# Second feed-forward product: the weight differences of Winograd's seven products made in other tiles

## The chip, the cores and the metric

The kernel runs on one core of a Trainium2 chip. The metric is the device time of one execution in microseconds (us), as the median over several runs. The engines that matter here are PE (TensorE, matrix products), ACT (ScalarE), DVE (VectorE), and SP (SyncE), which issues all the transfers. Each engine takes its instructions in a fixed order that was settled when the program was built, and an instruction that waits for another engine holds up everything behind it on its own engine.

## The reference, cut to what matters

One layer of a transformer-like trunk on 512 tokens of width 2048. Its last step is a gated feed-forward network, in float32:

```
h = rms_norm(x, norm2_g) * (1.0 + sc2) + sh2
gate, up = jnp.split(h @ w_ffn_in, 2, axis=-1)          # D_FF = 5632
x = x + g2 * ((jax.nn.silu(gate) * up) @ w_ffn_out)     # 5632 -> 2048
```

The change lies in the last product, `... @ w_ffn_out`, which is called the second product below. It takes the last 440 us or so of the execution.

## The kernel before

**Split numbers.** PE multiplies in a rounded 32-bit format. To keep float32 accuracy, each weight tile is split into a high and a low part: ACT copies it with rounding (`hi`, line 220), then DVE subtracts the copy from the tile (`lo`, line 221). Each block then needs three matmuls: high by high, low by high, high by low. The high tiles and the low tiles each have three rotating buffers, and every fourth split goes to a spare pair inside the tile `opsB`. So rows with `opsB` as a weight are splits like the others.

**Seven products instead of eight.** The second product is done by Winograd's form of Strassen's scheme: the four quarters of the weight block, y[0] to y[3], are combined to seven operands, and each is multiplied by a matching combination of the activations. Those were prepared earlier, lie in DRAM as `opd`, and come in as `opsA`, `opsB` and `opsC`. The order of the seven is `ORDER = (2, 1, 7, 6, 4, 5, 3)`. "Product 7" below is the one with that number, which comes third. Trace names count the place in the order from 0 and then the first block of a pair: `wfo6_2_0l` is unit 6, third product (7), blocks 0 and 1, low part.

**Units.** The 22 blocks of the inner dimension are cut into six chunks of 3, 3, 4, 4, 4 and 4 blocks, each done for two halves of the output columns. That gives 12 units, numbered 0 to 11. From unit 4 on a product is two pairs of blocks, or 24 matmuls.

**Sums.** Product 2 collects in the accumulators `foB`, products 7 and 4 in `foC`, products 1, 6, 5 and 3 all in the same two accumulators `foA` (one for each token half, called foA0 and foA1). After a product its result goes into the output tile `O`: mostly ACT copies it out (line 1210) and DVE adds the copy (line 1211). For product 3 DVE adds straight from `foA` (line 1275). The next unit's product 1 overwrites `foA`, so it may begin only when that add is done.

**Weight tiles and differences.** y[0] and y[2] of a unit come into a pool of four rotating buffers (`wfo`). y[1] and y[3] come into `yraw`, of which there is one for unit 0 and one for all the others. `T2` is a fifth tile of the same size, also one for all units after the first. `load_y` issues these loads on SP. y[1] and y[3] of the next unit have to wait until the present unit's last reader of the same tile is done. Before the change DVE makes four differences, each for pairs of blocks:

| for product | difference | line |
|---|---|---|
| 7 | y[0] becomes y[1] - y[0], all blocks ahead of the first split | 1254 |
| 7 | y[1] becomes y[3] - y[1] | 1190 |
| 6 | T2 becomes y[3] - y[0], with the new y[0] | 1190 |
| 4 | y[2] becomes y[2] - T2 | 1190 |

Product 1 takes the original y[0], so the first difference, which overwrites it, waits for product 1's split.

**What sets the order.** A scheduler in the framework places each engine's instructions by priority and by what it expects to be ready. Splits and differences have raised priority (`high_priority(offset=AHEAD)`), ACT's copies out of the accumulators have more; the adds into `O` have the ordinary one, so they go where the list has a gap.

Of the kernel before, what the change touches and what calls it, by code (L numbers as in the profile page):

```python
# [26 lines left out]
CHUNKS = (3, 3, 4, 4, 4, 4)  # L27
ORDER = (2, 1, 7, 6, 4, 5, 3)
AHEAD = 300
# [100 lines left out]
def trunk(ctx, tc, a):  # L130
    nc = tc.nc
    V, S, G = nc.vector, nc.scalar, nc.gpsimd
# [790 lines left out]
    for i, hs in enumerate(halves):  # L923
# [15 lines left out]
        y = rb[:, hs]  # L939
# [47 lines left out]
    for j in range(HALF):  # L987
        V.tensor_sub(block(0, 0, j), block(0, 1, j), block(0, 0, j))
        t2 = ft.tile([P, HT], F32, tag="t", name=f"t2_{j}")
# [34 lines left out]
    def place(n):  # L1024
        n %= 11
        return places[0][:, n] if n < 4 else places[1][:, n - 4] if n < 7 else places[2][:, n - 7]

    def load_op(c, q):
        if c < len(CHUNKS):
            nc.sync.dma_start(place(7 * c + q)[:, 0:CHUNKS[c]].bitcast(F32),  # L1030
                              opd[c][:, ORDER[q] - 1].rearrange("p n (h t) -> p n h t", h=2))

    def load_y(u, b):
        if u == len(units):
            return
        c, i = units[u]
        n = CHUNKS[c]
        t = raw_tile([P, n, T], f"wfo{u}_{b}") if b % 2 == 0 else yraw[u > 0][:, b // 2, 0:n]
        nc.sync.dma_start(t, a["w_fo"][i, b][:, starts[c]:starts[c] + n])
        blocks[u][b] = t  # L1040
# [142 lines left out]
    def multiply(out, c, q, raw, first, u, sums):  # L1183
        n = CHUNKS[c]
        x = place(7 * c + q)
        for k0 in range(0, n, 2):
            w = min(2, n - k0)
            with tc.high_priority(offset=AHEAD):
                for d, e, g in sums:
                    V.tensor_sub(*(t[:, k0:k0 + w] for t in (d, e, g)))  # L1190
            whi, wlo = split(raw[:, k0:k0 + w], [P, w, T], f"wfo{u}_{q}_{k0}")
            for j in range(2):
                js = slice(j * P, j * P + P)
                for kk in range(w):
                    k = k0 + kk
                    flags = dict(stop=False, skip_group_check=True)
                    PE.matmul(out[j], x[:, k, 0, js], whi[:, kk], start=first and k == 0, **flags)
                    PE.matmul(out[j], x[:, k, 0, js], wlo[:, kk], start=False, **flags)
                    flags["stop"] = k == n - 1
                    PE.matmul(out[j], x[:, k, 1, js], whi[:, kk], start=False, **flags)  # L1200

    def onto(dst, src, first):
        if first:
            with tc.high_priority(offset=2 * AHEAD):
                S.copy(dst, src)
            return
        t = cond[:, taps[0] % 4 * T:taps[0] % 4 * T + T]
        taps[0] += 1
        with tc.high_priority(offset=2 * AHEAD):
            S.copy(t, src)  # L1210
        V.tensor_add(dst, dst, t)
# [14 lines left out]
    def some_out(n):  # L1226
        for _ in range(min(n, len(outs))):
            emit_out(*outs.pop(0))

    for u, (c, i) in enumerate(units):  # L1230
        def dst(th, j, dh):
            return O[:, 2 * th + j, dh * 1024 + i * T:dh * 1024 + i * T + T]

        def ready(th, dh):
            if c == last_c:
                outs.extend((8 * dh + 4 * i + m, th) for m in range(4))

        first, final = c == 0, c == last_c
        if final and i == 0:
            for g in range(4):  # L1240
                nc.sync.dma_start(place(7 * c + 7 + g).bitcast(F32).rearrange("p n h t -> p n (h t)"), x1d[:, 4 * g:4 * g + 4])
        y = blocks[u]
        t2 = (T2 if u else yraw[0][:, 2])[:, 0:CHUNKS[c]]
        load_y(u + 1, 2)
        load_y(u + 1, 0)
        for q, p in enumerate(ORDER):
            out = {2: B[i], 7: C, 4: C}.get(p, A)
            raw = {2: y[2], 1: y[0], 7: y[1], 6: t2, 4: y[2], 5: y[0], 3: y[3]}[p]
            sums = {7: [(y[1], y[3], y[1])], 6: [(t2, y[3], y[0])], 4: [(y[2], y[2], t2)]}.get(p, ())
            if p == 7:  # L1250
                with tc.high_priority(offset=AHEAD):
                    for k0 in range(0, CHUNKS[c], 2):
                        ks = slice(k0, min(k0 + 2, CHUNKS[c]))
                        V.tensor_sub(y[0][:, ks], y[1][:, ks], y[0][:, ks])
            multiply(out, c, q, raw, p in (1, 7) or p == 2 and first, u, sums)
            if final:
                some_out(3)
            for j in range(2):
                if p == 1:
                    onto(dst(0, j, 0), A[j], first)  # L1260
                    if final:
                        V.tensor_add(dst(0, j, 0), B[i][j], dst(0, j, 0))
                elif p == 7:
                    onto(dst(1, j, 1), C[j], first)
                elif p == 6:
                    onto(dst(1, j, 0), A[j], first)
                elif p == 4:
                    V.tensor_add(dst(1, j, 0), C[j], dst(1, j, 0))
                elif p == 5:
                    onto(dst(1, j, 1), A[j], False)  # L1270
                elif p == 3:
                    if first:
                        S.copy(dst(0, j, 1), A[j])
                    else:
                        V.tensor_add(dst(0, j, 1), A[j], dst(0, j, 1))
            if p == 1:
                ready(0, 0)
                if final:
                    slots += [t[:, h * HT:h * HT + HT] for t in B[i] for h in range(2)]
            elif p in (4, 5, 3):  # L1280
                ready(*{4: (1, 0), 5: (1, 1), 3: (0, 1)}[p])
            if p == 7:
                load_y(u + 1, 1)
            if p == 3:
                load_y(u + 1, 3)
            if u == 0 and q == 6:
                places.append(hp.tile([P, 4, 4, 2, HT], F32R, tag="hhi", name="opsC"))
            if q < 4 and i == (c == 0):
                load_op(c + 1, q)
            if i == 1 and 1 <= q < 4:  # L1290
                load_op(c + 1, q + 3)
# [60 lines left out]
```

## Time and profile before

| | us |
|---|---|
| runs | 2299.24, 2299.24, 2306.46 (median 2299.24) |
| the profiled execution, its own time | 2301.37 |
| the profiled execution, span from the first to the last instruction | 2299.2 |
| PE busy | 2249.4 (98%) |
| DVE busy | 1917.8 (83%) |
| ACT busy | 1160.6 (50%) |

The span is the time from the first to the last instruction, and the execution's own time is 2.2 us more. PE is busy nearly throughout, so a change shows in the time only where it lengthens or shortens one of the few stretches in which PE waits, or adds matmuls. A timeline row gives the start and the length in us, the engine, the line, the operation, the tiles (buffer numbers left out), the shapes and the count. In brackets stands the idle time before it and what ended it. L93 is the helper that issues every matmul. Matmuls overlap: a row of one 128x512 matmul shows 0.39 us, while they follow each other every 0.227 us.

### The profile page before, as it was taken

The numbers are of one execution on the slowest core, as the hardware profiler recorded it, in microseconds if no ns is written. First come the engines' busy times: TensorE is split into PE (matmuls) and PEld (weight loads), VectorE is DVE, ScalarE is ACT, GpSimd is POOL, SyncE is SP. The second block draws the span as 40 slices with busy tenths as digits, with TensorE's granted clock in tenths as the row PEclk, the third lists the DMA queues.
The fourth block names the chain that finished last, engine by engine and source line by source line (L and its number), as shares of the span: only waits on it lengthen the run. The fifth ranks groups of instructions, "written<-read, shape, count | busy, mean of one in ns | idle before, by whom it ended". The sixth has DMA issues, their size and how long they took to land.

```text
span 2299.2 us, 35729 instructions
## 1 busy us (share of the span) xinstructions
PE 2249.4 (98%) x14171; PEld 2050.2 (89%) x14171; DVE 1917.8 (83%) x2566; ACT 1160.6 (50%) x2015; POOL 10.7 (0%) x25
## 2 busy tenths in 40 slices
PE   7999899999999999999999999999999999999999
PEld 6899899888888788999999999999999977778787
DVE  8887779999888865699899988888888778888888
ACT  4316666565655522564454445454545544544453
POOL 0000000000000000000000000000000000000000
PEclk9999999999999999999999999999999999999999
DMA  9885546853322386346555645454443486665452
GB/s 368 319 317 218 174 145 227 304 183 111 128 93 74 130 303 214 105 151 225 189 204 185 220 143 175 143 174 143 150 160 129 166 314 232 238 220 213 154 200 76
DMA packets 114978, 437.69 MB, mean 190 GB/s; under 512 B 9822, under 2 KB 58236, under 8 KB 76796
## 3 DMA queue, kind: packets, MB, share of 16 engines
q1 hardware_dynamic: 114812, 435.42, 53.0%
q8 instruction: 111, 1.82, 0.3%
q14 instruction: 55, 0.45, 0.1%
HBM read 386.61 MB, written 48.77 MB: 189 GB/s over the span
## 4 chain that ended last, share of the span: by engine, by line
PE 77%; DVE 13%; DMA 3%; issue 3%; ACT 3%; SPq 0%; DVEq 0%; ACTq 0%
PE ffA L93 18%; PE foA L93 9%; PE ffC L93 9%; PE sbp L93 7%; PE wo L93 7%; PE foC L93 4%; PE ffB L93 4%; PE st L93 4%; PE hgf L93 4%; PE hgq L93 3%; PE hgg L93 3%; DMA opd<-fhi 1%; DVE ada L180 1%; DVE yraw L1190 1%; PE l L93 1%
## 5 line engine op out<-in xcount | busy, mean ns | idle before, releaser
L180 DVE SCALAR_TENSOR_TENSOR ada<-ada,cond 128x2048 f32<-128x2048 f32 x95 | 216.8, 2286 | 54.5 <-DMA ada<-in_w_ada 54.3
L93 PE MATMUL ffA<-opD,ff_3h 128*128 128x256 f32 x512 | 93.9, 284 | 1.8 <-ACT u L1018 1.7
L93 PE MATMUL ffA<-opB,ff_6h 128*128 128x256 f32 x512 | 94.1, 284 | 1.0 <-ACT ff_6h L220 1.0
L93 PE MATMUL ffB<-opA,ff_2h 128*128 128x256 f32 x512 | 93.5, 283 | 0.0
L93 PE MATMUL ffC<-opC,ff_4h 128*128 128x256 f32 x512 | 93.5, 283 | 0.0
L93 PE MATMUL ffA<-opC,ff_5h 128*128 128x256 f32 x496 | 90.7, 283 | 0.8 <-ACT b L1018 0.8
L93 PE MATMUL ffA<-opA,ff_1h 128*128 128x256 f32 x496 | 90.6, 283 | 0.0
L93 PE MATMUL ffC<-opB,ff_7h 128*128 128x256 f32 x496 | 90.6, 283 | 0.0
L221 DVE TENSOR_TENSOR wfo_0l<-wfo,wfo_0h 128x1024 fp32r<-128x1024 f32 x48 | 58.7, 1224 | 37.9 <-ACT wfo_0h L220 37.5
L93 PEld LDWEIGHTS ffA<-opD,ff_3h 128*128 128x128 f32 x512 | 79.7, 192 | 2.4 <-ACT u L1018 2.4
L93 PEld LDWEIGHTS ffA<-opB,ff_6h 128*128 128x128 f32 x512 | 80.1, 193 | 1.3 <-ACT ff_6h L220 1.2
L93 PEld LDWEIGHTS ffC<-opC,ff_4h 128*128 128x128 f32 x512 | 79.7, 192 | 0.0
L93 PEld LDWEIGHTS ffB<-opA,ff_2h 128*128 128x128 f32 x512 | 79.7, 192 | 0.0
L220 ACT CAST wfo_0h<-wfo 128x1024 fp32r<-128x1024 f32 x48 | 50.6, 1054 | 57.5 <-PE foA L93 50.4
L1092 ACT CAST fhi<-forms 128x512 fp32r<-128x512 f32 (+1 forms) x63 | 43.6, 692 | 68.5 <-DMA opd<-fhi 59.2
L93 PEld LDWEIGHTS ffA<-opC,ff_5h 128*128 128x128 f32 x496 | 77.2, 192 | 1.0 <-ACT b L1018 1.0
L93 PEld LDWEIGHTS ffC<-opB,ff_7h 128*128 128x128 f32 x496 | 77.3, 192 | 0.0
L93 PEld LDWEIGHTS ffA<-opA,ff_1h 128*128 128x128 f32 x496 | 77.2, 192 | 0.0
L93 PE MATMUL ffA<-opB,ff_6l 128*128 128x256 f32 x256 | 72.7, 284 | 0.0
L93 PE MATMUL ffC<-opC,ff_4l 128*128 128x256 f32 x256 | 72.4, 283 | 0.0
L93 PE MATMUL ffA<-opD,ff_3l 128*128 128x256 f32 x256 | 72.4, 283 | 0.0
L93 PE MATMUL ffB<-opA,ff_2l 128*128 128x256 f32 x256 | 72.4, 283 | 0.0
(1646 smaller groups left out, 7764.6 us busy)
## 6 DMA issues: line engine op xcount, KB each, us to landing
ada<-in_w_ada SPq DMA_DIRECT2D x95, 1024.0 KB, 5.2
wfo<-in_w_fo SPq DMA_DIRECT2D x16, 1024.0 KB, 5.9
yraw<-in_w_fo SPq DMA_DIRECT2D x16, 1024.0 KB, 4.8
fix<-in_w_fix SPq DMA_DIRECT2D x14, 1024.0 KB, 5.6
opd<-forms SPq DMA_DIRECT2D x44, 256.0 KB, 4.3
opd<-fhi SPq DMA_DIRECT2D x42, 256.0 KB, 4.3
opsC<-opd SPq DMA_DIRECT2D x10, 1024.0 KB, 5.1
opsA<-opd SPq DMA_DIRECT2D x9, 1024.0 KB, 7.2
```

What stands on the lines that cost most here:

```text
L93: self.engine.matmul(out, lhsT, rhs, **kw)
L180: V.scalar_tensor_tensor(w, w, 1.0, row, op0=ALU.mult, op1=ALU.mult, accum_out=col)
L220: S.copy(hi, r)
L221: V.tensor_sub(lo, r, hi.bitcast(F32))
L1092: S.copy(hi, R[:, q])
L1190: V.tensor_sub(*(t[:, k0:k0 + w] for t in (d, e, g)))
```

## The change

Other tiles hold the differences. For product 7, y[3] - y[1] goes to T2 rather than over y[1], and then y[1] becomes y[1] - y[0]. For product 6, y[0] becomes y[3] - y[1], with the new y[1]. For product 4, y[2] becomes y[2] - y[0]. Product 5 takes y[1] where it took y[0]. The operands have the same values as before. There are four differences as before, but the loop that made the first of them for all blocks ahead is gone: both of product 7's are now made pair by pair inside `multiply`. Since y[1] is now read until product 5's split, the next unit's y[1] is loaded after product 5 rather than after product 7.

```diff
-            raw = {2: y[2], 1: y[0], 7: y[1], 6: t2, 4: y[2], 5: y[0], 3: y[3]}[p]
-            sums = {7: [(y[1], y[3], y[1])], 6: [(t2, y[3], y[0])], 4: [(y[2], y[2], t2)]}.get(p, ())
-            if p == 7:
-                with tc.high_priority(offset=AHEAD):
-                    for k0 in range(0, CHUNKS[c], 2):
-                        ks = slice(k0, min(k0 + 2, CHUNKS[c]))
-                        V.tensor_sub(y[0][:, ks], y[1][:, ks], y[0][:, ks])
+            raw = {2: y[2], 1: y[0], 7: t2, 6: y[0], 4: y[2], 5: y[1], 3: y[3]}[p]
+            sums = {7: [(t2, y[3], y[1]), (y[1], y[1], y[0])], 6: [(y[0], y[3], y[1])], 4: [(y[2], y[2], y[0])]}.get(p, ())
             multiply(out, c, q, raw, p in (1, 7) or p == 2 and first, u, sums)
...
-            if p == 7:
+            if p == 5:
                 load_y(u + 1, 1)
```

The scheduler answers with another order on the engines. In the rows below numbers tell tiles of one name apart, and the five lines of code taken out shift later line numbers: the add of line 1275 is line 1270 afterwards.

DVE at the head of unit 6, before, from product 1's first low part on; `O<-foA0` is the add of unit 5's product 3 from the first accumulator:

```order
L221 TENSOR_TENSOR wfo6_1_0l_20133<-wfo6_0_19844,wfo6_1_0h_20132 128x1024
L1275 TENSOR_TENSOR O_18741<-foA0_18742,O_18741 128x512
L1254 TENSOR_TENSOR wfo6_0_19844<-yraw_18716,wfo6_0_19844 128x1024
L221 TENSOR_TENSOR wfo6_1_2l_20149<-wfo6_0_19844,wfo6_1_2h_20148 128x1024
L1190 TENSOR_TENSOR yraw_18716<-yraw_18716 128x1024
L1254 TENSOR_TENSOR wfo6_0_19844<-yraw_18716,wfo6_0_19844 128x1024
L1190 TENSOR_TENSOR T2_18739<-yraw_18716,wfo6_0_19844 128x1024
L221 TENSOR_TENSOR wfo6_2_0l_20173<-yraw_18716,wfo6_2_0h_20172 128x1024
```

and with the change, from the same instruction:

```order
L221 TENSOR_TENSOR wfo6_1_0l_20133<-wfo6_0_19844,wfo6_1_0h_20132 128x1024
L1190 TENSOR_TENSOR T2_18739<-yraw_18716 128x1024 x2
L221 TENSOR_TENSOR wfo6_1_2l_20149<-wfo6_0_19844,wfo6_1_2h_20148 128x1024
L1190 TENSOR_TENSOR yraw_18716<-yraw_18716,wfo6_0_19844 128x1024
L221 TENSOR_TENSOR wfo6_2_0l_20172<-T2_18739,wfo6_2_0h_20171 128x1024
L1190 TENSOR_TENSOR yraw_18716<-yraw_18716,wfo6_0_19844 128x1024
L1190 TENSOR_TENSOR wfo6_0_19844<-yraw_18716 128x1024
L221 TENSOR_TENSOR opsB_18712<-T2_18739,opsB_18712 128x1024
L1190 TENSOR_TENSOR wfo6_0_19844<-yraw_18716 128x1024
L221 TENSOR_TENSOR wfo6_3_0l_20210<-wfo6_0_19844,wfo6_3_0h_20209 128x1024
L1190 TENSOR_TENSOR wfo6_2_19842<-wfo6_2_19842,wfo6_0_19844 128x1024 x2
L1270 TENSOR_TENSOR O_18741<-foA0_18742,O_18741 128x512
```

The add from foA0, second before, now comes after 13 instructions of 128x1024. Units 8 and 10 have the same order as unit 6. In units 5, 7 and 9 the first `T2` stands ahead of product 1's first low part, one of product 4's differences comes before product 6's low part, and 12 instructions from that low part on precede the add.

PE at the same place, before, from the end of product 2 to the beginning of product 7:

```order
L93 MATMUL foB01_18745<-opsB_18712,opsC_18951 128x512 x6
L93 MATMUL foA0_18742<-wfo6_1_0h_20132,opsA_18700 128x512
L93 MATMUL foA0_18742<-wfo6_1_0l_20133,opsA_18700 128x512
L93 MATMUL foA0_18742<-wfo6_1_0h_20132,opsA_18700 128x512 x2
L93 MATMUL foA0_18742<-wfo6_1_0l_20133,opsA_18700 128x512
L93 MATMUL foA0_18742<-wfo6_1_0h_20132,opsA_18700 128x512
L93 MATMUL foA0_18742<-wfo6_1_2h_20148,opsA_18700 128x512
L93 MATMUL foA0_18742<-wfo6_1_2l_20149,opsA_18700 128x512
L93 MATMUL foA0_18742<-wfo6_1_2h_20148,opsA_18700 128x512 x2
L93 MATMUL foA0_18742<-wfo6_1_2l_20149,opsA_18700 128x512
L93 MATMUL foA0_18742<-wfo6_1_2h_20148,opsA_18700 128x512
L93 MATMUL foC_18748<-wfo6_2_0h_20172,opsA_18700 128x512
```

and with the change, from the end of product 2 to the beginning of product 1:

```order
L93 MATMUL foB01_18745<-opsB_18712,opsC_18951 128x512 x6
L93 MATMUL foC_18748<-wfo6_2_0h_20171,opsA_18700 128x512
L93 MATMUL foC_18748<-wfo6_2_0l_20172,opsA_18700 128x512
L93 MATMUL foC_18748<-wfo6_2_0h_20171,opsA_18700 128x512 x2
L93 MATMUL foC_18748<-wfo6_2_0l_20172,opsA_18700 128x512
L93 MATMUL foC_18748<-wfo6_2_0h_20171,opsA_18700 128x512 x2
L93 MATMUL foC_18748<-wfo6_2_0l_20172,opsA_18700 128x512
L93 MATMUL foC_18748<-wfo6_2_0h_20171,opsA_18700 128x512 x2
L93 MATMUL foC_18748<-wfo6_2_0l_20172,opsA_18700 128x512
L93 MATMUL foC_18748<-wfo6_2_0h_20171,opsA_18700 128x512
L93 MATMUL foC_18748<-opsB_18712,opsA_18700 128x512 x12
L93 MATMUL foA0_18742<-wfo6_1_0h_20132,opsA_18700 128x512
```

Product 7 now goes ahead of all of product 1; before, product 1's half in foA0 went first. It is so in units 3 and 5 to 11.

DVE near the end of unit 0, before, where `wfo0_5_0l` is the first low part of unit 0's product 5 and `forms42` still belongs to the stage before:

```order
L1093 TENSOR_TENSOR forms42_18475<-forms42_18475,cond_72 128x512 x2
L1093 TENSOR_TENSOR forms42_18475<-forms42_18475,cond_72 128x768
L221 TENSOR_TENSOR wfo0_5_0l_18895<-wfo0_0_18705,wfo0_5_0h_18894 128x1024
L221 TENSOR_TENSOR wfo0_5_2l_18911<-wfo0_0_18705,wfo0_5_2h_18910 128x512
L221 TENSOR_TENSOR wfo0_6_0l_18925<-yraw0_18707,wfo0_6_0h_18924 128x1024
```

and with the change:

```order
L1093 TENSOR_TENSOR forms42_18475<-forms42_18475,cond_72 128x512 x2
L1093 TENSOR_TENSOR forms42_18475<-forms42_18475,cond_72 128x768
L1190 TENSOR_TENSOR T2_18739<-yraw_18716 128x1024
L1190 TENSOR_TENSOR T2_18739<-yraw_18716 128x512
L1190 TENSOR_TENSOR yraw_18716<-yraw_18716,wfo1_0_18751 128x1024
L1190 TENSOR_TENSOR yraw_18716<-yraw_18716,wfo1_0_18751 128x512
L221 TENSOR_TENSOR wfo0_5_0l_18894<-yraw0_18707,wfo0_5_0h_18893 128x1024
L221 TENSOR_TENSOR wfo0_5_2l_18910<-yraw0_18707,wfo0_5_2h_18909 128x512
L221 TENSOR_TENSOR wfo0_6_0l_18925<-yraw0_18707,wfo0_6_0h_18924 128x1024
```

Unit 1's four differences for product 7 now stand ahead of unit 0's product 5, and the first of them waits for the loads of unit 1's y[1] and y[3]. On SP the loads of y[1] for units 2 and later move back, past the next two `wfo` loads and up to three loads of activations, until they stand close to the load of y[3].

## The prediction, made before the changed kernel was run

> **What bounds the kernel now.** I read the page first, then PE's waits in the second product, then the timeline at one unit boundary.
>
> ```profile
> span 2299.2 us, 35729 instructions
> PE 2249.4 (98%) x14171; PEld 2050.2 (89%) x14171; DVE 1917.8 (83%) x2566; ACT 1160.6 (50%) x2015; POOL 10.7 (0%) x25
> ...
> PE 77%; DVE 13%; DMA 3%; issue 3%; ACT 3%; SPq 0%; DVEq 0%; ACTq 0%
> ```
>
> PE is the bound. No matmul is added or removed, so the time moves only by what PE waits. From the list of waits, second product alone:
>
> ```profile
> PE foA L93 <- ACT O L1205: 3.6, 1, 3.6
> PE foC L93 <- DVE wfo_0l L221: 2.4, 2, 1.3
> PE foC L93 <- DVE wfo_2l L221: 1.6, 3, 0.5
> PE foC L93 <- DVE opsB L221: 1.6, 3, 0.5
> ...
> PE foC L93 <- ACT wfo_0h L220: 0.3, 1, 0.3
> ```
>
> Columns: total, times, longest. All but the first are product 7 (foC) waiting for its low parts: two longer waits, in units 3 and 4, and six of 0.53, one in each of units 5 to 10. Together 5.9 us. That is what the change can win; the 3.6 us lie at unit 0's product 6, which it does not touch. Now the head of unit 6:
>
> ```profile
> 2048.50 0.39 PE L93 MATMUL foA<-wfo_2h,opsC 128*128 128x512 f32 x1
> 2049.78 1.23 DVE L221 TENSOR_TENSOR wfo_0l<-wfo,wfo_0h 128x1024 fp32r<-128x1024 f32 x1 [1.01 <-ACT wfo_0h L220]
> 2050.93 0.68 DVE L1275 TENSOR_TENSOR O<-foA,O 128x512 f32<-128x512 f32 x1
> 2051.22 0.39 PE L93 MATMUL foB<-wfo_0h,opsC 128*128 128x512 f32 x1
> 2053.79 1.22 DVE L1190 TENSOR_TENSOR yraw<-yraw 128x1024 f32<-128x1024 f32 x1
> 2056.06 1.22 DVE L1190 TENSOR_TENSOR T<-yraw,wfo 128x1024 f32<-128x1024 f32 x1
> 2056.66 0.39 PE L93 MATMUL foA<-wfo_0h,opsA 128*128 128x512 f32 x1
> 2059.38 0.39 PE L93 MATMUL foC<-wfo_0h,opsA 128*128 128x512 f32 x1
> 2061.74 1.22 DVE L221 TENSOR_TENSOR opsB<-yraw,opsB 128x1024 fp32r<-128x1024 f32 x1
> 2062.10 0.39 PE L93 MATMUL foC<-opsB,opsA 128*128 128x512 f32 x1
> 2063.01 2.83 PE L93 MATMUL foC<-opsB,opsA 128*128 128x512 f32 x11 [0.53 <-DVE opsB L221]
> 2065.15 0.68 DVE L1275 TENSOR_TENSOR O<-foA,O 128x512 f32<-128x512 f32 x1
> 2065.68 0.39 PE L93 MATMUL foA<-wfo_0h,opsA 128*128 128x512 f32 x1
> ```
>
> Read four things. PE does product 2's 24 matmuls in 2056.66 - 2051.22 = 5.44 us, 0.227 each. Between 2053.79 and 2065.15 DVE starts ten 128x1024 instructions, 1.136 us each, with no pause: DVE is the second bound here. Product 7's second low part (2061.74) comes too late, so the matmul due 0.227 after 2062.10 runs at 2063.01: PE loses 0.69. And the add from foA0 (2050.93), which must precede product 1 (2056.66), is done 5 us early.
>
> **The change, part by part.**
>
> *Work.* Four differences before, four after, same shapes: 0 us on DVE. The cover stays, since they still lie beside matmuls.
>
> *Units 6, 8, 10.* By the new order DVE does 13 instructions of 128x1024 from the row of 2049.78 on, then the add. PE runs product 7 where product 1 stood. Product 7 starts at 2056.66, its second half at 2059.38, that half's first low matmul is due at 2059.60. Its low part is DVE's ninth instruction: 2049.78 + 9 x 1.136 + 0.1 = 2060.1. PE waits 0.5 and is through with its remaining 11 matmuls at 2060.1 + 2.5 = 2062.6. Product 1 needs the add: 2049.78 + 13 x 1.136 + 0.68 = 2065.2. PE waits 2.6. In all 3.1 against 0.69: +2.4 each, +7.2 for three. The add lost its place because the difference that waited for product 1's split has gone, and with it the gap in the list.
>
> *Units 5, 7, 9.*
>
> ```profile
> 2003.86 0.33 SPq L1039 DMA_DIRECT2D yraw<-in_w_fo  x1
> ...
> 2008.41 1.23 DVE L221 TENSOR_TENSOR wfo_2l<-wfo,wfo_2h 128x1024 fp32r<-128x1024 f32 x1 [0.25 <-ACT wfo_2h L220]
> 2010.66 1.23 DVE L221 TENSOR_TENSOR wfo_0l<-wfo,wfo_0h 128x1024 fp32r<-128x1024 f32 x1 [1.02 <-ACT wfo_0h L220]
> 2012.09 0.39 PE L93 MATMUL foB<-wfo_0h,opsA 128*128 128x512 f32 x1
> 2017.53 0.39 PE L93 MATMUL foA<-wfo_0h,opsB 128*128 128x512 f32 x1
> ...
> 2023.89 0.50 PE L93 MATMUL foC<-wfo_2l,opsB 128*128 128x512 f32 x1 [0.53 <-DVE wfo_2l L221]
> ```
>
> The first T2 fills the 1.02 us pause before 2010.66. From there 12 instructions and the add: 2010.7 + 13.6 + 0.7 = 2025.0. Product 7 starts at 2017.53; its second low matmul, due at 2020.5, has its part at 2021.0, the ninth again. PE waits 0.5, is through at 2023.5, and waits 1.5 for the add. In all 2.0 against 0.69: +1.3 each, +3.9.
>
> *Unit 11* has the order of units 5 to 9 with output work between; I take +1.4, bounds 0 and 2.5.
>
> *Units 3 and 4.* Laid out the same way, product 7's waits go on about as before, since its low part still follows three differences. I take 0; bounds -3.0 (both longer waits gone) and +1.5 (as unit 5).
>
> *Units 0 and 1.* DVE gets unit 1's four differences ahead of unit 0's product 5, and the first needs unit 1's y[3].
>
> ```profile
> 1855.80 0.68 DVE L1190 TENSOR_TENSOR yraw<-yraw 128x512 f32<-128x512 f32 x1
> 1856.40 0.68 DVE L1190 TENSOR_TENSOR yraw<-yraw,wfo 128x512 f32<-128x512 f32 x1
> ...
> 1863.95 2.15 DVE L1093 TENSOR_TENSOR forms<-forms,cond 128x512 fp32r<-128x512 f32 x3
> 1868.45 0.81 SPq L1039 DMA_DIRECT2D yraw<-in_w_fo  x1
> 1871.13 1.23 DVE L221 TENSOR_TENSOR wfo_0l<-wfo,wfo_0h 128x1024 fp32r<-128x1024 f32 x1 [5.03 <-ACT wfo_0h L220]
> 1875.53 0.39 PE L93 MATMUL foA<-wfo_0l,opsB 128*128 128x512 f32 x1
> ```
>
> ```profile
> DMA to landing us min/median/max: 5.9/5.9/5.9
> ```
>
> The second fence is that load alone: issued at 1868.45 behind the last stores of the stage before, landed at 1874.4. Now DVE passes its pause of 5.03 us here waiting, does 1.14 + 0.60 + 1.14 + 0.60 = 3.5 us of differences (three blocks are a 128x1024 and a 128x512, and the latter follow each other after 0.60, first two rows), and makes product 5's low part at 1877.9 to 1879.1. PE wants it at 1875.53 and loses 3.6. Behind it on DVE stand the low parts of products 5 and 3, which PE reaches four microseconds later, in time. Bounds: 1.8 (load 1.8 quicker) and 5.4 (half clock, next).
>
> *Half clock.* Matmuls after a pause can run at half speed:
>
> ```profile
> 1012.00:1015.50 3.50, 1.62 (x11) 1.00 0.69 283
> 1015.50:1018.90 3.40, 3.40 (x18) 0.50 0.00 0
> ...
> 1865.40:1869.00 3.60, 3.57 (x9) 0.53 0.99 321
> 1968.00:2009.40 41.40, 40.12 (x175) 32.19 (x174) 36.02 (x38) 20.29 (x25) 0.00 (x0) 1.00 0.61 225
> ```
>
> The granted clock stands third from the end of a row. After the 3.6 us wait at unit 0, 9 matmuls took 3.60 instead of 2.04: 1.6 us lost. Unit 4, with a wait of 1.3, kept 1.00. And around 1012 to 1015.5 PE was busy 46% of 3.5 us, with no wait that long, and then ran at 0.50. So I add 1.6 in unit 1, and in units 6, 8 and 10, whose 2.6 us wait lies between the two cases, one and a half times 1.6 in total, 2.4; bounds 0 and 4.8.
>
> [...]
>
> *Loads.* y[1] of the next unit is issued after product 5's split rather than product 7's, close to y[3].
>
> ```profile
> yraw<-in_w_fo SPq DMA_DIRECT2D x16, 1024.0 KB, 4.8
> ```
>
> Issued with y[3] at the worst, y[1] lands 4.8 later: for unit 5 at 2008.7, and T2 starts at 2009.6 behind the row of 2008.41, so 0.9 to spare; for unit 6 some 3 us. The loads that it moves behind on SP have a whole product in hand. I take 0; later than 0.9 costs DVE the same in each odd unit.
>
> *Sum:* 7.2 + 3.9 + 1.4 + 0 + 3.6 + 1.6 + 2.4 = 20.1, and 0.11 for the slower first matmul after each of eight new waits (0.50 at 2023.89 against 0.39): about 21. The profiled execution has a span of 2299.2 and its own time is 2301.37; the median of the runs is 2299.24, 2.1 below that time. 2299.24 + 21 = 2320.
>
> **The rivals.**
>
> *Heavier.* The two loads meet others on the DMA engines and land 2 us later: 1.1 us in each of units 5, 7, 9 and 11, 4.4 in all, and all three even units run at half clock, 2.4 more: 2327. For it: `wfo` and `yraw` loads before shared the queue only sometimes, now two run together every unit. Against: 4.8 is the median of 16.
>
> *No change.* The new waits at product 1 stay out, because the add gets ahead, and only unit 1's 5.2 us are paid, against about half of product 7's 5.9: 2301.5. Against: the order puts the add last, on an engine that takes it in order.
>
> *Faster.* At product 1, units 5 to 11. If DVE's instructions followed each other every 0.9 us instead of 1.136, the add would be done in time (13 x 0.9 + 0.68 = 12.4, and 2049.78 + 12.4 is before 2062.6) and product 7 would never wait. If also unit 1's y[3] landed before DVE asks, 5.9 and eight slow restarts of about 0.27 go: -8.1, 2291 (0.27 is 0.69 - 0.53, and 0.11 by which the first matmul after a wait is longer, 0.50 against 0.39). It decides at 0.9. For it: nothing but that T2 spreads reads and writes over more tiles. Against: rows of line 1190 that write T2 or `yraw` show the same 1.22.
>
> *The change doesn't do what it says.* Product 7's first low part does come earlier, from eighth to sixth instruction in unit 6; only it was never the part PE waited for in units 5 to 10.
>
> **How the numbers follow.** Forecast 0.66, at 2320, own range 2312 to 2326 from the bounds of half clock, units 3, 4, 11 and unit 1. Heavier 0.15, no change 0.12, faster 0.07. About 0.3%, 7 us, is what a measurement of this kernel can tell from no change, so 2292.3 to 2306.1 counts as the same. The first two cases are slower: 0.81. The range 2306 to 2328 leaves out the faster case, most of no change and the tail of the heavier.
>
> **What would show it.** Right: PE's list of waits gains product 1 (foA) waiting for DVE's add, line 1270, about 1.5 and 2.6 us by turns in six units; a wait of some 3.5 us at foA for a low part near 1876, with DVE waiting for `yraw`'s load; in units 5 to 10 product 7 still waits about 0.5. Wrong: no such wait at 1270, or DVE's pace other than 1.136, or a granted clock of 1.00 throughout after 1880, which would take 2 to 4 us off.

## The result, and the profile after

The changed kernel takes 2318.66 us (median of 6 runs) where the kernel before takes 2303.38 (6 runs): a ratio of 1.0073, 95% interval 1.0057 to 1.0088, so 13 to 20 us more. The profiled execution has its own time 2316.51 and a span of 2314.3. First the head of its page and the chain that ended last.

```profile
span 2314.3 us, 35693 instructions
PE 2252.1 (97%) x14171; PEld 2048.7 (89%) x14171; DVE 1918.0 (83%) x2566; ACT 1163.4 (50%) x2015; POOL 10.7 (0%) x25
...
PE 75%; DVE 15%; DMA 4%; issue 3%; ACT 3%; SPq 0%; DVEq 0%; ACTq 0%
```

DVE is busy for 1918.0 us, before 1917.8: no work was added. What grew is waiting. PE's waits in the second product, changed kernel (what waited, on what, total, times, longest):

```profile
PE foA L93 <- DVE O L1270: 11.0, 7, 2.4
PE foA L93 <- DVE wfo_0l L221: 3.9, 2, 3.5
PE foA L93 <- ACT O L1205: 3.6, 1, 3.6
PE foB L98 <- DVE O L1222: 1.8, 3, 1.0
PE foC L93 <- DVE wfo_2l L221: 1.2, 3, 0.4
PE foC L93 <- DVE wfo_0l L221: 1.1, 1, 1.1
PE foC L93 <- DVE opsB L221: 1.1, 3, 0.4
PE foA L93 <- ACT cond L1210: 0.4, 1, 0.4
```

L98 is the helper that issues the output's transposes on PE. The first row is new: product 1 waits for the add of product 3, once for 0.29 us in unit 4 and six times for 1.2 or 2.35 in units 5 to 10. So is the 3.5 in the second row, at unit 0's product 5. Product 7 (foC) still waits, 3.4 us in all against 5.9 before. Now the head of unit 6 in the timeline, DVE first, then PE:

```profile
2053.36 1.23 DVE L221 TENSOR_TENSOR wfo_0l<-wfo,wfo_0h 128x1024 fp32r<-128x1024 f32 x1 [1.02 <-ACT wfo_0h L220]
2054.50 2.35 DVE L1190 TENSOR_TENSOR T<-yraw 128x1024 f32<-128x1024 f32 x2
...
2062.45 1.22 DVE L221 TENSOR_TENSOR opsB<-T,opsB 128x1024 fp32r<-128x1024 f32 x1
...
2068.12 1.28 DVE L1270 TENSOR_TENSOR O<-foA,O 128x512 f32<-128x512 f32 x2
```

```profile
2060.23 0.40 PE L93 MATMUL foC<-wfo_0h,opsA 128*128 128x512 f32 x1
2063.72 2.79 PE L93 MATMUL foC<-opsB,opsA 128*128 128x512 f32 x11 [0.36 <-DVE opsB L221]
2068.86 0.50 PE L93 MATMUL foA<-wfo_0h,opsA 128*128 128x512 f32 x1 [2.35 <-DVE O L1270]
```

From 2053.36 to the add lie 14.76 us, which is 13 x 1.136. PE could start product 1 at 2066.2 (eleven matmuls of 0.227 behind 2063.72) and stands until the first of the two adds is through.

Where the time lies by unit is read from windows that reach from one unit's first matmul to the next one's (length; busy time of PE, PEld, DVE, ACT, POOL; granted clock; DMA). Units 0, 5 and 6, before:

```profile
1849.43:1879.38 29.95, 26.38 (x110) 21.25 (x109) 21.66 (x30) 14.82 (x23) 0.00 (x0) 0.94 0.82 296
2012.09:2051.22 39.13, 38.60 (x170) 31.30 (x168) 33.27 (x35) 18.73 (x22) 0.00 (x0) 1.00 0.71 260
2051.22:2090.25 39.03, 38.50 (x170) 31.38 (x168) 33.18 (x35) 18.71 (x22) 0.00 (x0) 1.00 0.41 144
```

and after:

```profile
1846.57:1881.97 35.40, 28.29 (x111) 22.34 (x109) 24.96 (x34) 14.91 (x23) 0.00 (x0) 0.90 0.70 262
2014.24:2054.79 40.55, 38.95 (x170) 31.23 (x168) 32.25 (x34) 18.91 (x22) 0.00 (x0) 1.00 0.66 251
2054.79:2096.19 41.40, 38.69 (x170) 31.35 (x168) 34.33 (x36) 19.02 (x22) 0.00 (x0) 1.00 0.39 136
```

Unit 0 lost 5.45, unit 5 1.42, unit 6 2.37. Read the same way, units 5 to 10 lost 11.4 in all, unit 11 up to the end 1.6, and units 1 to 4 gained 0.4 together. That is 18.0 us from unit 0 on. The two spans differ by 15.1 only, because unit 0 began 2.86 earlier after (1846.57 against 1849.43), behind stages whose code the change does not touch.

### The profile page after: what moved, and what is told of

Its sections match the earlier page's. It is cut to its first block, busy times and chain, and to the rows that moved or that the text cites. A ratio compares the mean times of both kernels' runs of the same rounds, so it can differ in the third digit from the quotient of the medians.

```text
span 2314.3 us, 35693 instructions
## 1 busy us (share of the span) xinstructions
PE 2252.1 (97%) x14171; PEld 2048.7 (89%) x14171; DVE 1918.0 (83%) x2566; ACT 1163.4 (50%) x2015; POOL 10.7 (0%) x25
## 4 chain that ended last, share of the span: by engine, by line
PE 75%; DVE 15%; DMA 4%; issue 3%; ACT 3%; SPq 0%; DVEq 0%; ACTq 0%
PE ffA L93 17%; PE foA L93 8%; PE ffC L93 8%; PE sbp L93 7%; PE wo L93 7%; PE ffB L93 4%; PE st L93 4%; PE hgf L93 4%; PE hgq L93 3%; PE hgg L93 3%; PE foC L93 3%; DVE wfo L1190 2%; DVE wfo_0l L221 1%; DMA opd<-fhi 1%; DVE yraw L1190 1%
```

## The experiments

Two questions stood. Is it the order on DVE that costs, or has DVE too little time, so that any order would wait somewhere? And what put the add last? All ratios are to the kernel before, run on the same chip.

**Adds first.** In the changed kernel:

```
                    else:
-                        V.tensor_add(dst(0, j, 1), A[j], dst(0, j, 1))
+                        with tc.high_priority(offset=2 * AHEAD):
+                            V.tensor_add(dst(0, j, 1), A[j], dst(0, j, 1))
```

> The changed kernel, with the two adds of product 3 (line 1270) given priority over DVE's differences and splits. Theory (the order on DVE is what costs): the seven waits at these adds, 11.0 us, go; product 7's seven short waits, 3.4 us, go or halve, since the scheduler must put the splits closer to their use; the 3.5 us wait at unit 0's product 5 and its half clock (1.7) stay. Time: 11 to 15 below the changed kernel, which is between 4 below and 4 above the kernel before. Rival (DVE has too little time in the second product, so that a wait pushed out of one place comes back at another): product 7's waits grow by what the adds' waits lose, and the time stays within 4 us of the changed kernel, 12 or more above the kernel before.

Measured: 2296.13 (12 runs), 0.9979 (0.9969 to 0.9989), by the ratios some 22 us below the changed kernel and 5 below the one before. PE's waits of this kernel in the second product, whole:

```profile
PE foA L93 <- DVE wfo_0l L221: 4.4, 1, 4.4
PE foA L93 <- ACT O L1205: 3.6, 1, 3.6
PE foB L98 <- DVE O L1257: 1.5, 1, 1.5
PE foB L98 <- DVE O L1222: 1.0, 1, 1.0
```

All seven waits at the adds are gone, and product 7's with them. Unit 0's wait stayed, here with 4.4. DVE does the same work and PE waits for it nowhere in units 1 to 9; the 1.5 is new, at the transposes of unit 10's output. The rival of too little time falls. More came back than the 11 to 15 expected. In the profiles units 1 to 11 take 21.6 less than in the changed kernel; the waits explain 14.5 of it. Some 4 more are slow restarts behind the waits: each time 0.16 beyond the idle time that the profile shows and 0.11 at the next matmul (the row of 2068.86 starts 2.74 behind the matmul ahead of it, where 0.227 + 2.35 is 2.58). The remaining 3 or so were not traced.

**Unit 1 old.** In the changed kernel, unit 1 alone makes its differences as before:

```
+            if u == 1:
+                raw = {2: y[2], 1: y[0], 7: y[1], 6: t2, 4: y[2], 5: y[0], 3: y[3]}[p]
...
+            else:
+                raw = {2: y[2], 1: y[0], 7: t2, 6: y[0], 4: y[2], 5: y[1], 3: y[3]}[p]
...
```

> The changed kernel, with unit 1 alone making its differences as the kernel before does. Theory: the 3.5 us wait at unit 0's product 5 near 1876 goes, and with it the stretch at half clock behind it (1.7 us): 5 us below the changed kernel, about 10 to 12 above the kernel before; the waits at the adds stay at 11 us. Rival (the wait comes from the load of y[3], late behind the stage before, so that whoever first uses it waits): the same wait stands at another matmul of unit 0 or 1, and the time stays within 2 us of the changed kernel.

Measured: 2315.19 (6 runs), 1.0058 (1.0046 to 1.0070). The 3.5 us wait at unit 0's product 5 is gone and stands nowhere else, and unit 0 takes 31.27 in place of 35.40. So the load was not late for others; the differences stood too early. But the gain in the second product was a little under 4, not 5: here the stretch at half clock behind the 3.58 us wait at product 6 (granted clock 0.50 from 1865.9 to 1872.0) went on for 14 matmuls, in the changed kernel (0.50 from 1863.05 to 1866.47) for 9. The 95% intervals of this ratio and of the changed kernel's overlap, so by time alone this run shows little; the wait and the unit show it.

**Both edits.**

> Both edits: the adds of product 3 first, and unit 1 in the old form. Theory: the effects add, 16 to 20 below the changed kernel, so from 1 above to 5 below the kernel before, with no wait of PE over 1 us after the 3.6 us at unit 0's product 6. Rival (too little time on DVE): the waits come back at product 7, 8 or more above the kernel before.

Measured: 2291.53 (6 runs), 0.9954 (0.9942 to 0.9966). The effects add: by the ratios 5.8 us beyond the adds alone. PE's waits are the 3.6 at unit 0's product 6 and 1.0 at the end. The time expected was from 1 above to 5 below the kernel before; it is 10 below.

**Adds first, in the kernel before.** The same edit at line 1275.

> The kernel before, with the two adds of product 3 given the same priority. There the adds are done 5 us ahead of their use and nobody waits for them. If only the adds' own place matters, nothing changes: within 2 us of the kernel before, and product 7's waits stay at 5.9 us. If the place of the adds in the scheduler's list also decides where it puts the splits behind them, product 7's waits shrink, by up to 5.9 us and 2 us of slow restarts: 5 to 8 below the kernel before, and then the gain of the adds-first edit isn't owed to the other tiles.

Measured: 2291.41 (5 runs), 0.9953 (0.9941 to 0.9965): without the other tiles as much as both edits gave with them, though nobody waited for these adds. What went are product 7's waits, down from 5.9 us to 0.3:

```profile
PE foC L93 <- DVE wfo_0l L221: 0.3, 1, 0.3
```

In this profile another 1.6 comes from unit 0, where the same wait of 3.58 was not followed by half clock (granted clock 1.00 from 1867.2 to 1871.2); no edit brought that about. PE's rows in unit 6 tell why product 7 waits no more:

```profile
2051.98 0.39 PE L93 MATMUL foA<-wfo_0h,opsA 128*128 128x512 f32 x1
...
2057.42 0.39 PE L93 MATMUL foC<-wfo_0h,opsA 128*128 128x512 f32 x1
...
2062.86 0.39 PE L93 MATMUL foA<-wfo_0h,opsA 128*128 128x512 f32 x1
```

PE does all 24 matmuls of product 1 (5.44 us), then product 7, then product 6. In the kernel before it began product 7 2.72 us after product 1 (2059.38 - 2056.66), since the second half of product 1 writes foA1, whose add stood on DVE only at 2065.15; that half came behind product 7. So the scheduler builds three orders on PE: half of product 1 first (before), product 7 first (after), all of product 1 first (adds first, in either kernel). Only the last gives product 7's low parts 5.4 us of cover in place of 2.7 or none, and with it their waits are all but gone. Given to the second add alone, the priority makes the scheduler build the very same program, so the second add alone is enough.

**Gap kept.** In the changed kernel the difference of y1 and y0 goes into y0 again, which must wait for product 1's split; product 7 still uses T2:

```
-            raw = {2: y[2], 1: y[0], 7: t2, 6: y[0], 4: y[2], 5: y[1], 3: y[3]}[p]
-            sums = {7: [(t2, y[3], y[1]), (y[1], y[1], y[0])], 6: [(y[0], y[3], y[1])], 4: [(y[2], y[2], y[0])]}.get(p, ())
+            raw = {2: y[2], 1: y[0], 7: t2, 6: y[1], 4: y[2], 5: y[0], 3: y[3]}[p]
+            sums = {7: [(t2, y[3], y[1]), (y[0], y[1], y[0])], 6: [(y[1], y[3], y[0])], 4: [(y[2], y[2], y[1])]}.get(p, ())
```

> The changed kernel, with the difference y1 - y0 written into y0 again, so that it waits for product 1's split as before; only product 7's first difference goes to T2 and is free. If the prediction's reason holds (the add lost its place because the waiting difference, and with it the gap in DVE's list, was gone), the adds stand early again: no wait at line 1270 over 0.5 us, 9 or more below the changed kernel. Rival (one free difference for product 7 is enough: PE's list takes product 7 ahead of product 1, and the adds, which nothing calls for early any more, slide behind the splits): the waits of about 1.2 and 2.4 us by turns stay, within 3 us of the changed kernel but for what unit 1 does near 1876, where only a part of the 3.5 us stays, since fewer differences can run ahead there.

Measured: 2318.40 (4 runs), 1.0067 (1.0053 to 1.0081), the same as the changed kernel. Its waits:

```profile
PE foA L93 <- DVE O L1270: 11.2, 8, 2.4
...
PE foA L93 <- DVE wfo_0l L221: 2.4, 2, 2.0
PE foC L93 <- DVE wfo_0l L221: 1.7, 1, 1.7
```

The waiting difference is back, and the waits at the add stay. PE in unit 6 still begins product 7 first:

```profile
2060.07 0.39 PE L93 MATMUL foC<-wfo_0h,opsA 128*128 128x512 f32 x1
...
2068.70 0.49 PE L93 MATMUL foA<-wfo_0h,opsA 128*128 128x512 f32 x1 [2.35 <-DVE O L1270]
```

So the rival held: one free difference for product 7 is enough to move it ahead of product 1 on PE and to leave the adds behind. That the total is the same is chance, at least in the profile: unit 0 takes 3.1 less than in the changed kernel, and units 6 and 8 take 1.6 and 1.5 more. In unit 6 the granted clock was 0.50 from 2070.6 to 2073.2; what unit 8 lost its time by is not shown.

**The load alone**, moved in the kernel before (`if p == 7:` to `if p == 5:`).

> The kernel before, with nothing changed but the place of the load of y[1] of the next unit, after product 5 in place of product 7. Theory (loads have time to spare): within 2 us of the kernel before, and product 7's waits as before, 5.9 us. Rival (two 1 MB loads close together land later and hold up the first difference): 4 or more above.

Measured: 2302.75 (10 runs), 1.0003 (0.9994 to 1.0012), with every wait of the second product as before. In the kernel before, the moved load costs nothing.

**Differences without priority.** Line 1190's `high_priority(offset=AHEAD)` becomes `offset=0` in the changed kernel; the kernel before gets the same, there and at line 1254's group.

> The changed kernel, with no priority for the differences in line 1190 in place of 300; splits keep theirs. Theory (the differences' priority puts them ahead of what PE needs first): adds, splits and unit 0's product 5 all come ahead of them, every wait of PE after unit 0 is under 0.5 us; the time is that of the run with both edits (adds first, unit 1 in the old form) or up to 5 below it, 10 to 15 below the kernel before. Rival (differences without priority come too late for product 7 and product 6): waits of 1 us or more at foC or foA for their splits in most of units 2 to 11, so 5 or more above the run with both edits.

> The kernel before, with no priority for its differences (line 1190 and line 1254). If the other tiles of the change bring anything once the order is right, this stays above the changed kernel with the same edit, by the waits for product 1's split: 3 to 6 us above it. If they bring nothing, the two agree within 2 us.

Measured: the changed kernel 2287.54 (5 runs), 0.9929 (0.9916 to 0.9941), which beats both kernels and lies, by the ratios, some 6 below the run with both edits, about as expected; the kernel before 2293.42 (5 runs), 0.9962 (0.9949 to 0.9976). First the waits of the changed kernel with this edit, then those of the kernel before with it:

```profile
PE foA L93 <- ACT O L1205: 1.7, 1, 1.7
PE foB L98 <- DVE O L1222: 1.0, 1, 1.0
```

```profile
PE foA L93 <- ACT O L1205: 3.6, 1, 3.6
PE foC L93 <- DVE wfo_0l L221: 1.2, 2, 0.9
PE foB L98 <- DVE O L1222: 1.0, 1, 1.0
```

And units 0, 5 and 6 of the first:

```profile
1849.94:1876.52 26.58, 24.84 (x110) 20.06 (x109) 22.67 (x31) 15.01 (x23) 0.00 (x0) 1.00 0.89 335
2004.82:2042.90 38.08, 38.08 (x169) 31.54 (x168) 32.15 (x34) 18.83 (x22) 0.00 (x0) 1.00 0.69 255
2042.90:2080.98 38.08, 38.08 (x169) 31.54 (x168) 33.96 (x36) 19.05 (x22) 0.00 (x0) 1.00 0.45 160
```

Units 5 and 6 take 38.08, which is 168 matmuls of 0.2267: PE never stands. Here the changed kernel stays ahead by the 3 to 6 us that the last expectation allowed, but not only by waits for product 1's split. The waits explain 1.9 at unit 0's product 6 and 1.2 at product 7, with about 0.5 of restarts, of the 5.9 us between the two medians. The profiles are 5.8 apart, and 1.9 of that was already there when unit 0 began (1849.94 against 1851.82). Why those stages took less time is open; no experiment looked at them. So some 3.6 us can be put down to the other tiles and the order that follows from them, and the rest cannot.

## Why the prediction was right, and where not

- *Time and sign.* 2320 forecast, 2318.66 measured. The forecast started from a median of 2299.24 that six runs put at 2303.38, so the rise was 15.3, not 21. In the profiles, from unit 0 on, it is 18.0. That the time itself came out within 1.4 us is luck in part: the starting point was 4.1 too low and the rise 5.7 too large.
- *Units 6, 8, 10.* +2.4 each forecast, 2.37, 2.39 and 2.34 measured. Thirteen instructions of 1.136 and the add set the end, as worked out.
- *Units 5, 7, 9.* +1.3 each forecast; 1.42, 1.39 and 1.45 measured. Product 7 still waits there, 0.36 to 0.39, where 0.5 was forecast. *Unit 11:* +1.4 forecast, 1.6 measured, though not by a wait at line 1270: 0.8 of it are waits at the transposes (line 1222), and the rest was not traced. *Units 3 and 4:* 0 forecast, -0.3 and -0.1 measured.
- *Unit 0.* The wait was 3.5 where 3.6 stood in the sum. DVE's row shows what it waited for, T2's first difference for the load of y[3]:

```profile
1871.64 1.83 DVE L1190 TENSOR_TENSOR T<-yraw 128x1024 f32<-128x1024 f32 x2 [8.39 <-DMA yraw<-in_w_fo]
...
1876.39 0.54 PE L93 MATMUL foA<-wfo_0l,opsB 128*128 128x512 f32 x1 [3.53 <-DVE wfo_0l L221]
```

- *Half clock.* This term was mis-sized. The 1.6 in unit 0 came, nine matmuls at a granted clock of 0.55, first row below. The 2.4 in units 6, 8 and 10 did not: behind each wait of 2.35 the clock stayed at 1.00, for unit 6 in the second row. Without it the sum is 17.7, or 18.6 with the restarts, against 18.0.

```profile
1876.30:1880.10 3.80, 3.71 (x9) 2.97 (x10) 3.57 (x6) 0.00 (x0) 0.00 (x0) 0.55 0.18 23
2068.80:2072.30 3.50, 3.44 (x15) 2.88 (x16) 3.00 (x5) 0.93 (x2) 0.00 (x0) 1.00 0.00 0
```

- *The reason given for the add's place* was wrong: "the difference that waited for product 1's split has gone, and with it the gap in the list". With that difference kept waiting, the adds stood as late. What goes with the late adds in these runs is PE's order: in units 5 to 10 they stand late where product 7 goes ahead of product 1, in the changed kernel and in the one with the gap kept, and nobody waits for them where product 1, or its first half, goes first. That the adds slid to where PE next asks for them is the likely reading; no run shows which of the two the scheduler settles first. The size was right because it was read from the order as built.
- *Rivals.* The heavier one fell: the load alone, moved in the kernel before, changed nothing, and units 5, 7 and 9 lost 1.4, not 2.4. "No change" fell with the waits at line 1270. "Faster" needed a quicker DVE; DVE's pace stayed at 1.136. The prediction did not see that the waits could be had back by order alone, in either kernel.

## What to carry to other kernels

A wait that is taken off one engine may be what held the scheduler to a good order on another: look at what now comes first on both before counting the gain. Where an instruction that nobody waits for sits late in a queue, as the second add did, see whether it also decides what the next engine may take first. When preparatory work has a priority of its own, try it without: here it took 9 us off the kernel before, and some 33 off the changed one (by the ratios), while moving the tiles alone cost some 15.

## What the runs showed of the hardware

The half clock is less regular than the prediction took it. Eleven pauses of 3.53 to 4.35 us were seen between 1862 and 1881 in nine profiles, and nine were followed by matmuls 0.43 apart, 8 to 14 of them; two, of 3.58 us (adds first, in the kernel before: granted clock 1.00 from 1867.2 to 1871.2) and 3.62 (the kernel before without priority: matmuls 0.23 apart), were not. In the trace of the kernel before the granted clock is 0.50 from 1865.41 to 1868.83, and the pause ends at 1865.43. In that of the changed kernel it is 0.50 from 1863.05 to 1866.47 and from 1876.71 to 1880.12, 0.48 and 0.32 behind the ends of its two pauses (1862.57 and 1876.39). These three stretches last 3.4 us. With unit 1 old and with both edits the clock was at 0.50 for at least 6.1 and 5.3 us (1865.9 to 1872.0, 1867.3 to 1872.6).

Of five pauses of 2.35 us (units 6, 8 and 10 of the changed kernel, unit 6 with unit 1 old and with the gap kept), one was followed by half clock, that with the gap kept. There the matmuls stand 0.43 apart from 1.3 us after the pause on; most of that stretch is this row:

```profile
2070.60:2073.20 2.60, 2.60 (x7) 1.98 (x7) 1.04 (x2) 0.13 (x1) 0.00 (x0) 0.50 0.00 0
```

Pauses of 1.74 us (the changed kernel without priority, granted clock 1.00 throughout unit 0) and 2.02 us (gap kept, matmuls 0.23 apart behind it) left the clock alone. The cost of a pause at one place in the program thus varied by some 3 us between these runs (14 matmuls by 0.2, or none). The same pause of 3.58 us was followed by half clock in seven profiles and not in an eighth; no run shows what decides it.
